# A transformer trunk layer on one core: the first feed-forward projection as a product of seven block products, with the engines' order written out

## The chip, the core and the metric

The kernel runs on one core of a Trainium2 chip. The metric is the device time of one execution in microseconds (us). Before the change it is 1105.56 us, the median of three runs from 1104.16 to 1106.84. A difference under 0.2% (2.2 us) is taken as none.

Engines are named as in the profile: PE (TensorE matmul), PEld (TensorE weight load), DVE (VectorE), ACT (ScalarE), POOL (GpSimd), SP (SyncE, which issues the loads).

## What is computed

One trunk layer with shared weights for 512 latent and 128 context tokens, 640 in all, model width 1024, feed-forward width 2816, float32. The part that the change touches is the second half of the layer:

```python
x = x + gate1 * (merged @ w_out)
h = modulate(x, norm2_w, shift2, scale2)       # RMSNorm(x) * (1 + scale2) + shift2
a, up = jnp.split(h @ w_ffn_in, 2, axis=-1)    # 1024 -> 2 x 2816
a = dwconv3(a, ffn_conv_w, ffn_conv_b)         # three taps along the tokens
x = x + gate2 * ((jax.nn.silu(a) * up) @ w_ffn_out)
```

Both groups of tokens end with a final RMSNorm. The vectors gate1, shift2, scale2 and gate2 come from products of a small condition vector with `w_ada`.

## The kernel before, in words

**Number format.** A float32 operand is held as two `F32R` tiles, `hi` (an ACT copy) and `lo` (operand minus hi, a DVE subtraction), and a product takes three matmuls: hi*hi, hi*lo and lo*hi. `wload` (line 117) and `wcols` (line 130) load 512 KB of weights from SP into a tile `raw` (three buffers), then make `whi` and `wlo` (four buffers each). `mm` (line 141) issues a matmul; where `pinned` is set, `pin` keeps the order of the program text on PE, and the other engines' instructions are placed by the scheduler.

**PSUM.** Eight banks: `bank2` (line 103) hands out pairs of banks in a turn of three, `bank1` single banks in a turn of two.

**Output projection.** For each of five blocks `t` of 128 tokens, `out_steps(t)` (line 1013) multiplies `mg` with `w_out` in 8 contraction blocks, three matmuls each, and both column halves: 48 matmuls of 512 columns. The first two blocks alternate. Behind the matmuls DVE multiplies by gate1, adds to `x2[t]`, ACT squares, and DVE scales by the reciprocal root. `modulate(t)` (line 1033) turns the block with eight PE transposes, applies scale2 and shift2 (four operations on DVE, four on ACT) into `h32`, and splits it into `h2[0]` and `h2[1]`. It stands inside the matmuls of the next block, behind its sixth contraction block.

**First feed-forward projection.** The 640 tokens are two halves of 320 (`HALF`), the contraction is 8 blocks of 128. For each of 22 tiles `i` of 128 columns, `ffn_tile` (line 1083) has `ffn_proj` (line 985) compute the tile of `a` (`pfa`) and the tile of `up` (`pfu`): per tile and operand 8 blocks x 3 matmuls x 2 halves = 48 matmuls of 128x320. Three half projections (`ffn_half`, `early`) run before the last `modulate`. ACT copies `pfa` to `av` and applies the middle tap into `cv`; DVE adds the other two taps (four `scalar_tensor_tensor`, 511 and 127 columns), ACT applies silu, DVE multiplies by `pfu`, ACT and DVE split the product into hi and lo of the gated tile (`gA`, `gB`).

**Second feed-forward projection.** Tiles go in two groups of 11 (`GRP`, line 1074). After a group, its gated tiles are multiplied with `w_ffn_out` for two column halves `hf`, in five accumulators `acc` of 512 columns, and DVE adds `acc * g2` to `x2`. `gate2` (line 1076) gets gate2 by `ada_acc` (line 208): 1024 rows of `w_ada` times the condition, 16 `scalar_tensor_tensor` on DVE per column half; one step of it runs behind each of the first tiles. In the very last half `finish` (line 1102) applies the final norm and stores.

Of the kernel before, what the change touches and what calls it, by code (L numbers as in the profile page):

```python
# [67 lines left out]
def trunk_kernel(ctx: ExitStack, tc: tile.TileContext, a: dict, o: list):  # L68
# [72 lines left out]
    def mm(out, s, m, start, stop):  # L141
        pin(nc.tensor.matmul(out, s, m, start=start, stop=stop))  # L142
# [65 lines left out]
    def ada_acc(pool, col, hf, name):  # L208
# [3 lines left out]
        acc = pool.tile([P, 2, 512], F32, tag="acc", name=f"acc_{name}{hf}", bufs=2)  # L212
# [3 lines left out]
        for u in range(4):  # L216
            raw = wpool.tile([P, 2, 512], F32, tag="raw", name=f"raw_{name}{hf}{u}", bufs=3)
            nc.sync.dma_start(raw, w_ada[2 * u * P:(2 * u + 2) * P, c0:c0 + 512].rearrange("(k p) n -> p k n", p=P))
            for ki in range(2):
                for c in range(2):  # L220
                    nc.vector.scalar_tensor_tensor(acc[:, c, :], raw[:, ki, :], sc[:, c, 2 * u + ki:2 * u + ki + 1],  # L221
                                                   acc[:, c, :], ALU.mult, ALU.add)
# [16 lines left out]
    def rows_cols(pool, ps):  # L239

        rows = pool.tile([8, 512], F32, tag="n2rows", name="n2rows", bufs=1)
# [731 lines left out]
    h2 = mg  # L973
    tail = ctx.enter_context(tc.tile_pool(name="tail", bufs=1, reuse_waits="tile"))
    x2 = [tail.tile([P, D], F32, tag=f"x2_{t}", name=f"x2_{t}") for t in range(NT)]
    g2 = [tail.tile([P, D], F32, tag=f"g2_{c}", name=f"g2_{c}") for c in range(2)]

    def ffn_half(i, u):

        w = wcols(w_fi, u * FF + i * P, P, 0, KD, f"f{'au'[u]}{i}")  # L980
        ps = bank2(f"pf{'au'[u]}{i}")
        proj(ps, w, h2, KD, halves=(0,))
        return ps, w

    def ffn_proj(i, u):
        if (i, u) in early or i < 2:
            ps, w = early.get((i, u)) or ffn_half(i, u)
            proj(ps, w, h2, KD, halves=(1,))
            return ps
        w = wcols(w_fi, u * FF + i * P, P, 0, KD, f"f{'au'[u]}{i}")  # L990
        ps = bank2(f"pf{'au'[u]}{i}")
        proj(ps, w, h2, KD)
        return ps

    early = {}
    with tc.tile_pool(name="wo", bufs=1, reuse_waits="tile") as wo:
# [3 lines left out]
        woB = [wo.tile([P, 3, D], F32R, tag=f"woB{i}", name=f"woB{i}") for i in range(2)]  # L1000

        def wo_of(i, k):
            return woA[i][:, k, :] if k < 5 else woB[i][:, k - 5, :]

        for k in range(KD):
            raw = wpool.tile([P, 1024], F32, tag="raw", name=f"raw_wo{k}", bufs=3)
            nc.sync.dma_start(raw, w_out[k * P:(k + 1) * P, :])
            nc.scalar.copy(wo_of(0, k), raw)
            nc.vector.tensor_tensor(wo_of(1, k), raw, f(wo_of(0, k)), ALU.subtract)
# [3 lines left out]
        def out_steps(t):  # L1013
# [3 lines left out]
            for k in range(KD):  # L1017
                for i, (s, m) in enumerate(((0, 0), (0, 1), (1, 0))):
                    for b in range(2):
                        mm(ps[:, b, :], mg[s][:, k, ts], wo_of(m, k)[:, b * 512:(b + 1) * 512],  # L1020
                           k == 0 and i == 0, k == KD - 1 and i == 2)
                if k % 2 and k < KD - 1:
                    yield
            y = Y2[t] = wo.tile([P, D], F32, tag="y", name=f"y{t}", bufs=2)
            for b in range(2):
                nc.vector.tensor_tensor(y[:, b * 512:(b + 1) * 512], ps[:, b, :], g1[b][:, t // 4, :], ALU.mult)
            nc.vector.tensor_tensor(x2[t], x2[t], y, ALU.add)
            ss = wo.tile([P, 1], F32, tag="ss", name=f"ss2_{t}", bufs=4)
            nc.scalar.activation(y, x2[t], AF.Square, accum_out=ss)
            r = rstd_of(wo, ss, f"n2_{t}")  # L1030
            nc.vector.tensor_scalar(y, x2[t], r, None, ALU.mult)

        def modulate(t):
            c, ts, y = t // 4, slice(t * P, (t + 1) * P), Y2[t]
            h32 = wo.tile([P, KD, P], F32, tag="h32", name=f"h32_{t}", bufs=1)
            for q in range(2):
# [3 lines left out]
                for j in range(4):  # L1040
                    kk = 4 * q + j
                    src, s_, b_ = pt[:, j * P:(j + 1) * P], modc["sc2"][:, kk, c:c + 1], modc["sh2"][:, kk, c:c + 1]
                    if j % 2:
                        nc.scalar.activation(h32[:, kk, :], src, AF.Identity, bias=b_, scale=s_)
                    else:
                        nc.vector.tensor_scalar(h32[:, kk, :], src, s_, b_, ALU.mult, ALU.add)
            n = KD if t < NT - 1 else KD // 2
# [154 lines left out]
```

## Time and profile before

| | us |
|---|---|
| median of three runs | 1105.56 |
| the profiled execution | 1108.31 |
| its span, first to last instruction | 1106.5 |
| PE busy in the span | 1071.1 (97%) |
| DVE busy | 701.2 (63%) |
| ACT busy | 486.5 (44%) |
| POOL busy | 163.0 (15%) |
| mean granted clock of TensorE, share of full | 0.991 |

The span begins with the first instruction and ends with the last; the profiled execution's own time is 1.8 us longer. Busy time of an engine is the union of its instructions. A matmul's row shows its whole latency, and matmuls overlap, so the pace of a run of matmuls is read from the chain, which gives the length of a stretch and how many matmuls it holds. In an idle note such as `[6.60 <-DVE ks L578]` the engine stood for 6.60 us until the named instruction ended.

### The profile page before, as it was taken

Reading aid. Unit: us, or ns where it says so; the run is one execution under the profiler, and the core shown is the slowest. Engines: PE = TensorE matmul, PEld = TensorE weight load, DVE = VectorE, ACT = ScalarE, POOL = GpSimd, SP = SyncE. Lnnn points to the kernel's source line nnn. Section 1 sums busy time; section 2 is a strip of 40 time slices with the busy share of each in tenths; the row PEclk is TensorE's granted clock in tenths of the full one; section 3 lists DMA queues with packets and bytes.
Section 4 is the critical chain, followed back from the end, with each engine's and each line's share of the span. In section 5 each row is a group of like instructions: output and inputs, shape, how many; then the busy total and the mean of one; then the engine's idle time right before and its main releaser. Section 6 shows DMA issues by size and latency. Waiting matters only on the chain.

```text
span 1106.5 us, 16752 instructions
## 1 busy us (share of the span) xinstructions
PE 1071.1 (97%) x6811; PEld 1006.3 (91%) x6811; DVE 701.2 (63%) x1041; ACT 486.5 (44%) x783; POOL 163.0 (15%) x160
## 2 busy tenths in 40 slices
PE   6988999999999999999999999999999999999997
PEld 4787899999999999999998899999988999999886
DVE  5968988988877577787756567564414444444164
ACT  8636667667665552222334444333311233333133
POOL 4444324323222630000000000000000000000020
PEclk9898999999999999999999999999999999999999
DMA  9830212112111124555565024241222222222212
GB/s 311 228 97 27 84 32 65 48 37 66 41 42 58 55 81 152 171 156 150 153 220 161 1 80 141 86 133 58 86 76 76 87 77 76 77 77 68 67 39 95
DMA packets 128478, 106.10 MB, mean 96 GB/s; under 512 B 4173, under 2 KB 110205, under 8 KB 128402
## 3 DMA queue, kind: packets, MB, share of 16 engines
q1 hardware_dynamic: 126450, 101.93, 29.9%
q0 software_dynamic: 1232, 1.80, 0.8%
q8 instruction: 53, 0.87, 0.3%
q10 hardware_dynamic: 720, 1.31, 0.3%
q14 instruction: 23, 0.19, 0.1%
HBM read 101.36 MB, written 3.67 MB: 95 GB/s over the span
## 4 chain that ended last, share of the span: by engine, by line
PE 80%; DVE 11%; ACT 4%; issue 2%; SPq 1%; DMA 1%; ACTq 0%; DVEq 0%
PE pfa L142 14%; PE pfu L142 14%; PE acc L142 13%; PE ps_g L142 10%; PE psyb L142 5%; PE pso L142 5%; PE psk L142 3%; PE psu L142 3%; PE psya L142 3%; PE s L142 2%; PE po L142 2%; PE psq L142 2%; DVE nm L667 2%; PE psv L142 2%; PE pat L145 1%
## 5 line engine op out<-in xcount | busy, mean ns | idle before, releaser
L142 PE MATMUL pfu<-mg,whi_fu 128*128 128x320 f32 x704 | 134.1, 308 | 0.0
L142 PE MATMUL pfa<-mg,whi_fa 128*128 128x320 f32 x704 | 134.1, 308 | 0.0
L142 PEld LDWEIGHTS pfa<-mg,whi_fa 128*128 128x128 f32 x704 | 110.9, 188 | 0.4
L142 PEld LDWEIGHTS pfu<-mg,whi_fu 128*128 128x128 f32 x704 | 110.7, 188 | 0.0
L142 PE MATMUL acc<-whi_fo,gA 128*128 128x512 f32 (+1 forms) x336 | 100.9, 379 | 0.0
L142 PE MATMUL ps_g<-hT,whi_g 128*128 128x320 f32 x512 | 96.7, 311 | 0.0
L142 PE MATMUL pfu<-mg,wlo_fu 128*128 128x320 f32 x352 | 82.2, 307 | 0.0
L142 PE MATMUL pfa<-mg,wlo_fa 128*128 128x320 f32 x352 | 82.2, 307 | 0.0
L142 PEld LDWEIGHTS ps_g<-hT,whi_g 128*128 128x128 f32 x512 | 80.2, 188 | 2.0 <-issue 1.5
L126 DVE TENSOR_TENSOR wlo_fo<-raw_fo,whi_fo 128x1024 fp32r<-128x1024 f32 (+1 forms) x24 | 27.3, 1145 | 80.8 <-ACT whi_fo L125 80.8
L669 ACT ACTIVATE p<-s,nm 128x640 f32<-128x640 f32 (+1 forms) x80 | 56.6, 709 | 40.0 <-DVE nm L667 39.4
L142 PEld LDWEIGHTS acc<-whi_fo,gA 128*128 128x128 f32 x336 | 62.1, 188 | 12.1
L126 DVE TENSOR_TENSOR wlo_fa<-raw_fa,whi_fa 128x1024 fp32r<-128x1024 f32 x22 | 26.9, 1224 | 66.3 <-ACT whi_fa L125 66.3
L1176 POOL TENSOR_TENSOR x<-x,fw 128x512 f32<-128x512 f32 x5 | 6.9, 1372 | 419.0 <-ACT sq L1175 419.0
L142 PE MATMUL psv<-whi_v,hT 128*128 128x256 f32 x320 | 66.4, 288 | 0.0
L125 ACT CAST whi_fo<-raw_fo 128x1024 fp32r<-128x1024 f32 (+1 forms) x24 | 23.3, 978 | 96.3 <-PE acc L142 71.3
L667 DVE TENSOR_REDUCE nm<-s 128x1 f32<-128x640 f32 (+1 forms) x80 | 56.5, 709 | 12.4 <-PE s L142 11.0
L142 PE MATMUL acc<-wlo_fo,gA 128*128 128x512 f32 (+1 forms) x168 | 63.7, 379 | 0.0
L125 ACT CAST whi_fa<-raw_fa 128x1024 fp32r<-128x1024 f32 x22 | 23.1, 1050 | 84.8 <-PE pfa L142 61.7
L221 DVE SCALAR_TENSOR_TENSOR acc_g<-raw_g,silu,acc_g 128x512 f32<-128x512 f32 x64 | 44.5, 746 | 24.8 <-DMA raw_g<-in_w_ada_dram 24.7
L142 PEld LDWEIGHTS pfu<-mg,wlo_fu 128*128 128x128 f32 x352 | 59.4, 188 | 0.0
L142 PEld LDWEIGHTS pfa<-mg,wlo_fa 128*128 128x128 f32 x352 | 59.4, 188 | 0.0
(337 smaller groups left out, 2576.3 us busy)
## 6 DMA issues: line engine op xcount, KB each, us to landing
raw_fa<-in_w_ffn_in_dram SPq DMA_DIRECT2D x22, 512.0 KB
raw_fu<-in_w_ffn_in_dram SPq DMA_DIRECT2D x22, 512.0 KB
raw_fo<-in_w_ffn_out_dram SPq DMA_DIRECT2D x20, 512.0 KB
raw_g<-in_w_in_dram SPq DMA_DIRECT2D x16, 512.0 KB
raw_g<-in_w_ada_dram SPq DMA_DIRECT2D x16, 512.0 KB
araw_sh<-in_w_ada_dram SPq DMA_DIRECT2D x8, 512.0 KB
araw_sc<-in_w_ada_dram SPq DMA_DIRECT2D x8, 512.0 KB
raw_v<-in_w_in_dram SPq DMA_DIRECT2D x8, 512.0 KB
```

Source lines behind the costliest of these rows:

```text
L125: nc.scalar.copy(hi[:, :n], rv)
L126: eng.tensor_tensor(lo[:, :n], rv, f(hi[:, :n]), ALU.subtract)
L142: pin(nc.tensor.matmul(out, s, m, start=start, stop=stop))
L145: pin(nc.tensor.transpose(out, x, ident))
L221: nc.vector.scalar_tensor_tensor(acc[:, c, :], raw[:, ki, :], sc[:, c, 2 * u + ki:2 * u + ki + 1], acc[:, c, :], ALU.mult, ALU.add)
L667: nc.vector.tensor_reduce(nm[:, i:i + 1], s, AX.XY, ALU.max, negate=True)
L669: nc.scalar.activation(p.rearrange("p (b n) -> p b n", b=s.shape[1]), s, AF.Exp, bias=nm[:, i:i + 1], accum_out=z[:, i:i + 1])
L1176: nc.gpsimd.tensor_tensor(x2[t][:, hs], x2[t][:, hs], fw[:, hs], ALU.mult)
```

## The change

1. The first projection is one product of blocks of two by two: the weight tile of `a` (k blocks 0 to 3 and 4 to 7) and that of `up` (the same), against `h` cut into k blocks 0 to 3 and 4 to 7 and token halves 0 and 1. It takes seven block products of 12 matmuls (4 k blocks x 3) of 128x320, numbered 1 to 7 in `product`, in place of eight. The sums on the token side are made once in `modulate` (`e1` to `e4`, kept in `h2` and in the new tile `hx`). The sums on the weight side are made per tile by POOL (`sums`, four operations of 512 columns). Per tile the weights take four hi/lo pairs (`hilo` 1 to 4: three of 1024 columns and one of 512). Sums of the products are made in PSUM where they can be (`pa` collects 1, 6, 7, 4; `pc` 5 and 3) and by DVE (`add2`, `add7`, `add3`).
2. DVE, ACT and POOL instructions of this stage go through `Pin`, which keeps them in the order of the text. `start` writes out the first three tiles, `cycle` the others.
3. The tiles go in groups of 8, 7 and 7. The last two products of a group's last tile stand behind the first blocks of the second projection, and `prepare` readies the next group's first tile in its last block.
4. `gate2` is stepped twice behind each block of the second projection of group 0; half of its sums go to ACT and POOL (`part`). The load of the final norm's weight `fw`, issued by POOL, moves from the start of the stage to the second projection of the last group.
5. The output projection of blocks 2 to 4 goes one PSUM bank after the other (`by_half`), so that `half(0)` follows its first bank. `modulate(t-1)` stands behind contraction block 8 of the first bank (behind block 7 for the last), `modulate(0)` behind block 1.

The core of the diff:

```diff
+    dve, act, pool = Pin(nc.vector), Pin(nc.scalar), Pin(nc.gpsimd)
...
+    def load(i, u, dst=None):
+        raw = R[i, u] = dst if dst is not None else wpool.tile([P, KD, P], F32, tag="raw", ..., bufs=3)
+        nc.sync.dma_start(raw, w_fi[:, c0:c0 + P].rearrange("(k p) n -> p k n", p=P))
+    def sums(i, b, dst=None):
+        ra, ru = R[i, 0], R[i, 1]
+        s = S[i, b] = dst if dst is not None else pools["ffn"].tile([P, KD, P], F32, tag="s", ...)
+        if b == 0:
+            pool.tensor_tensor(s[:, :4, :], ru[:, :4, :], ru[:, 4:, :], ALU.add)
+            pool.tensor_tensor(s[:, 4:, :], s[:, :4, :], ra[:, :4, :], ALU.subtract)
+        else:
+            pool.tensor_tensor(s[:, :4, :], ra[:, 4:, :], S[i, 0][:, 4:, :], ALU.subtract)
+            pool.tensor_tensor(s[:, 4:, :], ra[:, :4, :], ru[:, :4, :], ALU.subtract)
+    def hi(i, n):
+        src = {1: lambda: R[i, 0], 2: lambda: S[i, 0], 3: lambda: S[i, 1], 4: lambda: R[i, 1][:, 4:, :]}[n]()
+        if n < 4:
+            w = [wpool.tile([P, KD, P], F32R, tag=t, ...) for t in ("whi", "wlo")]
+            for p, k0 in zip(((1, 2), (5, 6), (3, 7))[n - 1], (0, 4)):
+                W2[i, p] = [x[:, k0:k0 + 4, :] for x in w]
+        act.copy(w[0], src)
+    def lo(i, n, eng=dve):
+        eng.tensor_tensor(l, src, f(h), ALU.subtract)
+    def product(i, *ps):
+        for p in ps:
...
+            out = {1: pa, 6: pa, 7: pa, 4: pa, 5: pc, 3: pc, 2: PB.get(i)}[p]
+            (wh, wl), (ah, al) = W2.pop((i, p)), h_block(p)
+            for k in range(4):
+                for n, (w, x) in enumerate(((wh, ah), (wh, al), (wl, ah))):
+                    mm(out, w[:, k, :], x[:, k, :], p in (1, 2, 5) and k + n == 0, k == 3 and n == 2, p in (6, 7, 4, 3))
...
         def modulate(t):
+            free = dve if t == NT - 1 else pool
...
+            dve.tensor_tensor(e1, b12, h1[:, :4, cs], ALU.subtract)
+            dve.tensor_tensor(e2, b22, e1, ALU.subtract)
+            split_to(h2[0][:, :4, c2], h2[1][:, :4, c2], e1)
+            free.tensor_tensor(e3, b22, b12, ALU.subtract)
+            yield
+            split_to(hx[0][:, :4, cs], hx[1][:, :4, cs], e2)
+            split_to(h2[0][:, 4:, c2], h2[1][:, 4:, c2], b22, free)
+            yield
+            free.tensor_tensor(e4, h1[:, 4:, cs], e2, ALU.subtract)
+            split_to(hx[0][:, 4:, cs], hx[1][:, 4:, cs], e[:, 8:, :n], free)
...
+            for n in out_steps(t, True):
+                if n == (7, 7, 6)[t - 2]:
+                    each(modulate(t - 1))
+                elif t == 2 and n == 0:
+                    each(modulate(0))
+                elif t == NT - 1 and n in (2, 10):
+                    hilo(n // 8, 1, pool)
+                elif t == NT - 1 and n == 14:
+                    hi(2, 1)
...
+        lo(2, 1, pool)
+        product(0, 1, 2)
+        product(1, 1)
+        copy1(0, spare[0][:, 7, :])
+        add2(0)
+        sums(0, 0, room(0, 2))
+        rest = modulate(NT - 1)
+        next(rest)
+        product(2, 1)
+        product(1, 2)
+        hilo(0, 2)
+        sums(0, 1, room(1, 2))
+        next(rest)
+        product(2, 2)
+        hilo(0, 3)
+        each(rest)
...
+    def cycle(i, first, end):
+        j, n = (i - 1 if i > first else None), (i + 1 if i < end else None)
...
+        product(i, 1, 2)
+        do(j, lambda j: product(j, 7))
+        do(j, add3)
+        do(j - 1 if j is not None and j > first else None, glo)
+        do(j, conv)
+        copy1(i)
+        do(n, sums, 0)
+        do(n, hi, 2)
+        add2(i)
+        do(n, lo, 2)
+        do(j, silu)
+        do(j, add7)
+        do(j, glu2)
+        do(n, hi, 1)
+        product(i, 5)
+        do(n, sums, 1)
+        copy5(i)
+        do(n, lo, 1)
+        do(n, hi, 4)
+        do(n, lo, 4)
+        product(i, 6)
+        if i + 2 <= end:
+            load(i + 2, 0)
+        copy6(i)
+        do(n, hi, 3)
+        do(j, lambda j: product(j, 4))
+        do(j, glu1)
+        do(n, lo, 3)
+        product(i, 3)
+        if i + 2 <= end:
+            load(i + 2, 1)
...
+    def start():
+        product(0, 5, 6)
+        load(2, 1)
+        copy5(0)
+        sums(1, 0)
+        sums(1, 1)
+        hilo(1, 2)
+        copy6(0)
+        product(0, 3, 7)
...
+        hilo(0, 4)
+        hilo(1, 4)
+        product(1, 5, 6)
...
+        product(0, 4)
...
+        product(1, 3, 7)
...
+        product(2, 5, 6)
...
+        product(1, 4)
...
+        product(2, 3)
...
+        out2 = blocks()
+        next(out2)
+        product(end, 7)
+        add7(end)
+        glu2(end)
+        next(out2)
+        product(end, 4)
+        glu1(end)
+        glo(end)
+        each(out2)
```

`add2`, `add7`, `add3` and `glu1` are one DVE operation of 320 columns with one operand in PSUM, `glu2` one of 320 columns and `glo` one of 640 with both in SBUF. `copy1`, `copy5` and `copy6` are ACT copies of 320 columns from PSUM. `conv` is the old middle tap on ACT and the old four operations on DVE. `hilo` is `hi` and `lo`.

## Rows read from the trace of the kernel before

**Rows 1.** The page, engines: busy us, share of the span, instructions

```profile
PE 1071.1 (97%) x6811; PEld 1006.3 (91%) x6811; DVE 701.2 (63%) x1041; ACT 486.5 (44%) x783; POOL 163.0 (15%) x160
```

**Rows 2.** The page, chain that ended last, shares of the span by line

```profile
PE pfa L142 14%; PE pfu L142 14%; PE acc L142 13%; PE ps_g L142 10%; PE psyb L142 5%; PE pso L142 5%; PE psk L142 3%; PE psu L142 3%; PE psya L142 3%; PE s L142 2%; PE po L142 2%; PE psq L142 2%; DVE nm L667 2%; PE psv L142 2%; PE pat L145 1%
```

**Rows 3.** Groups of `pfa` (`pfu` has the same): count, busy us, mean ns, idle

```profile
L142 PE MATMUL pfa<-mg,whi_fa 128*128 128x320 f32 x704 | 134.1, 308 | 0.0
...
L142 PE MATMUL pfa<-mg,wlo_fa 128*128 128x320 f32 x352 | 82.2, 307 | 0.0
```

**Rows 4.** Chain in order of time: start us, length us, matmuls in it

```profile
611.31 11.11 PE pso L142 x48
...
709.12 7.04 PE pfa L142 x48
...
912.42 6.99 PE pfa L142 x48
```

**Rows 5.** Tiles 11 to 21: length, busy of PE, PEld, DVE, ACT, POOL, clock

```profile
870.50:1024.20 153.70, 153.70 (x1057) 153.70 (x1057) 67.78 (x95) 53.87 (x66) 0.00 (x0) 1.00 0.26 78
```

**Rows 6.** The same stretch, groups of DVE: count, busy us, mean ns

```profile
L126 DVE TENSOR_TENSOR wlo_fu<-raw_fu,whi_fu 128x1024 fp32r<-128x1024 f32 x10 | 12.2, 1218 | 0.0
L1091 DVE SCALAR_TENSOR_TENSOR cv<-av,vcol,cv 128x511 f32<-128x511 f32 (+1 forms) x22 | 11.2, 550 | 1.7 <-ACT cv L1089 1.5
...
L1098 DVE TENSOR_TENSOR gA<-cv,gA 128x640 fp32r<-128x640 f32 x8 | 6.6, 819 | 0.0
```

**Rows 7.** Groups of ACT by form: count, busy us, mean ns, idle

```profile
L125 ACT CAST whi_fu<-raw_fu 128x1024 fp32r<-128x1024 f32 x22 | 23.1, 1048 | 45.3 <-PE pfu L142 18.1 <-PE pfa L142 14.5 <-PE acc L142 5.7
L1089 ACT ACTIVATE cv<-pfa,vcol 128x640 f32<-128x640 f32 x22 | 19.6, 889 | 0.0
...
L1095 ACT ACTIVATE cv<-cv 128x640 f32<-128x640 f32 x22 | 16.3, 739 | 47.3 <-DVE cv L1093 47.2
...
L736 ACT COPY u<-psu 128x320 f32<-128x320 f32 x4 | 1.7, 419 | 0.0
```

**Rows 8.** Timeline, POOL with DVE: operands all in SBUF, then DVE reading PSUM

```profile
1066.90 1.29 POOL L1176 TENSOR_TENSOR x<-x,fw 128x512 f32<-128x512 f32 x1 [1.44 <-ACT sq L1175]
...
1066.92 1.81 DVE L1172 TENSOR_TENSOR x<-x,yr 128x512 f32<-128x512 f32 x1
...
73.99 2.85 POOL L126 TENSOR_TENSOR wlo_q<-raw_q,whi_q 128x1024 fp32r<-128x1024 f32 x1
76.81 1.74 POOL L541 TENSOR_TENSOR ry_k<-ry_k,cos 128x512 f32<-128x512 f32 x1
...
74.50 2.89 DVE L542 TENSOR_TENSOR rsh_k<-rsh_k,sin 128x512 f32<-128x512 f32 x1
...
355.46 2.68 POOL L748 TENSOR_TENSOR s<-s 128x669 f32<-128x669 f32 x2 [0.42 <-DVE u L759]
...
355.49 2.35 DVE L693 TENSOR_TENSOR tl<-pat,th 128x1024 fp32r<-128x1024 f32 x2
```

**Rows 9.** Operations of line 1172: shortest, middle and longest in ns

```profile
L1172 DVE TENSOR_TENSOR x<-x,yr x15: 681/689/1812, 832.7 to 1072.4; 128x512 f32<-128x512 f32 x15
```

**Rows 10.** A weight load: its issue, then microsecond stretches ending in DMA share, GB/s

```profile
914.51 0.37 SPq L122 DMA_DIRECT2D raw_fa<-in_w_ffn_in_dram  x1
...
917.00:918.00 1.00, 1.00 (x9) 1.00 (x8) 0.00 (x0) 0.00 (x0) 0.00 (x0) 1.00 0.56 167
918.00:919.00 1.00, 1.00 (x9) 1.00 (x8) 0.00 (x0) 0.00 (x0) 0.00 (x0) 1.00 0.00 0
```

**Rows 11.** Timeline, `modulate` near the end of the output projection

```profile
634.84 1.78 DVE L1046 TENSOR_SCALAR h<-pt,sc,sh 128x128 f32<-128x128 f32 x4 [2.68 <-PE pt L145]
```

**Rows 12.** PE after a long idle time, and engines and clock in two stretches

```profile
86.45 0.60 PE L142 MATMUL s<-ks,qd 128*128 128x320 f32 x1 [6.60 <-DVE ks L578]
...
80.00:85.00 5.00, 0.00 (x0) 0.00 (x0) 4.87 (x7) 3.13 (x5) 3.57 (x3) 0.89 0.00 1
85.00:90.00 5.00, 3.54 (x14) 3.58 (x15) 4.68 (x6) 1.31 (x4) 0.63 (x1) 0.50 0.00 0
```

More of the change, by code (lines that the diff above doesn't have):

```diff
@@ new lines, in copy1, with add2, copy5, copy6 @@
+    def copy1(i, dst=None):
+        AV[i] = dst if dst is not None else pools["ffn"].tile([P, TOK], F32, tag="av", name=f"av{i}")
+        act.copy(AV[i][:, :HALF], PS[i][:, 0, :HALF])
+    def add2(i):
+        dve.tensor_tensor(AV[i][:, :HALF], AV[i][:, :HALF], PB.pop(i), ALU.add)
+    def copy5(i):
+        C22[i] = pools["ffn"].tile([P, HALF], F32, tag="c22", name=f"c22_{i}")
+        act.copy(C22[i], PS[i][:, 1, :HALF])
+    def copy6(i):
+        act.copy(AV[i][:, HALF:], PS[i][:, 0, :HALF])
@@ L1027, in out_steps @@
[L1027 to L1031, printed above, removed]
+                if n == len(order) - 1:
+                    continue
+                yield n
+                if n == KD - 1:
+                    half(0)
+            if not by_half:
+                half(0)
@@ new lines, in prepare, with do @@
+    def prepare(i):
+        load(i, 0)
+        load(i, 1)
+        sums(i, 0)
+        hilo(i, 1)
+        sums(i, 1)
+        hilo(i, 2)
+        hilo(i, 4)
+        load(i + 1, 0)
+        hilo(i, 3)
+        load(i + 1, 1)
+    def cycle(i, first, end):
+        j, n = (i - 1 if i > first else None), (i + 1 if i < end else None)
+        def do(tile, op, *args):
+            if tile is not None:
+                op(tile, *args)
+        product(i, 1, 2)
[29 more added lines that the diff above has]
+            load(i + 2, 1)
@@ new lines, in trunk_kernel, with blocks @@
+    later = gate2()
+    for g, (first, size) in enumerate(GROUPS):
+        end = first + size - 1
+        if g == 0:
+            start()
+        else:
+            gates_of(g)
+        for i in range(3 if g == 0 else first, end + 1):
+            cycle(i, first, end)
+        add3(end)
+        glo(end - 1)
+        conv(end)
+        silu(end)
+        def blocks():
+            for hf in range(2):
+                for _ in out2_steps(g, hf):
+                    yield
+                    if g == 0:
+                        next(later, None)
+                        next(later, None)
+        out2 = blocks()
[8 more added lines that the diff above has]
+        each(out2)
```

345 lines of the change are left out of this document (223 added, 122 removed).

## The prediction

> **What bounds the kernel now.** I read the page's engine line first: PE is busy for 97% of the span [rows 1]. Then the chain that ended last: `pfa` and `pfu`, the two operands of the first feed-forward projection, hold 28% of it [rows 2]. Their groups give the count: 704 + 352 matmuls for `pfa`, as many for `pfu`, 2112 in all, with no idle time in front [rows 3]. A matmul's row shows latency (308 ns), so the pace comes from the chain in order of time: 48 matmuls in 7.04 or 6.99 us, 146.7 or 145.6 ns each [rows 4]. Last, the stretch of tiles 11 to 21: PE works 153.70 of 153.70 us at full clock, 13.97 us a tile, while DVE works 67.78, ACT 53.87 and POOL nothing [rows 5]. So only PE's work costs time here, and the question is whether the other engines' new work stays under what is left of PE's.
>
> **Matmuls removed: 38.5 us less.** Seven products of 12 matmuls for 22 tiles are 1848, 264 fewer than 2112. At 145.6 to 146.7 ns that is 38.4 to 38.7 us. A product takes 1.75 us, a tile 12.24.
>
> The Trainium skill, "TensorE: Matmul & The Clock Gate", Back-to-back issue gap, states some 81 ns a matmul at 128 columns and 131 at 512 in a sustained stream; a straight line between them is an estimate of 106 ns at 320, which would make the saving 28 us and the end 1104. The trace has 231 ns at 512 columns (48 in 11.11 us) [rows 4], so its own pace is used.
>
> **The repeating cycle: 11.9 us more.** Per tile DVE gets three subtractions of 1024 columns at 1.22, one of 512 at 0.69, the convolution (four operations, 2 x 11.2 / 11 = 2.04 a tile), one of 640 at 0.82, and five of 320, by the step from 512 to 640 some 0.49 each [rows 6, 9]: 9.7 us, against 6.1 before. ACT gets three copies at 1.05, one of 512 (some 0.6), a tap at 0.89, silu at 0.74, the gated copy (some 0.73) and three copies of 320 at 0.42: 7.4 [rows 7]. POOL gets four sums at 1.29: 5.2 [rows 8]. Each is under 12.24, but they don't run side by side. Where POOL and a DVE operation with both operands in SBUF meet, the second stands still: DVE began 0.02 us behind POOL, took 1.81 in place of 0.69 and ended 0.54 after it; POOL, caught the same way, ended 1.16 after DVE [rows 8, 9]. DVE reading PSUM isn't held: two such operations took 2.35 us under two of POOL [rows 8].
>
> I walk one cycle with these (0 is the start of product 1; *n* is the next tile, *j* the one before). The loop settles at 13.1 us. The last weights of *n* go into the buffer that `lo(n-1,1)` freed near 11.0 of the cycle before; a load takes some 3.1 us from issue (914.51 to about 917.6) [rows 10], so they land near 1.2. DVE ends `lo(.,3)` at 0.4, `add3` at 0.8, `glo` at 1.5; ACT's tap lets the convolution begin at 1.7. POOL takes the port at 1.5, and its four sums then alternate with the four taps: first sum until 2.65, taps of 0.55, 0.55, 0.17, 0.17 (the last two by length), three sums of 1.15: the convolution ends at 7.5, where 2.04 would have ended it near 3.8. `add2` ends at 7.9, `lo(n,2)` at 9.1, `add7` at 9.55. Product 4 adds onto the bank that `add7` reads, and PE stands before it from 8.75 (five products): 0.85 us. Nothing else stops PE: `hi(n,1)` must wait for product 6 to give back its `whi` buffer, ends at 9.9, and `lo(n,1)` at 11.05 is in time for 13.1; `copy5` ends at 10.3, before product 3. Queued behind the late convolution are on ACT silu (until 8.3), on DVE all the rest; POOL's sums delay nobody but DVE. Only tiles with a successor in their group do sums: 4 + 5 + 5 = 14, so 11.9 us. Bounds: 0, if the sums fall into DVE's waits and PSUM operations; 2.35 a tile, 33 us, if DVE's 9.7 and POOL's 4 x 1.16 never overlap and the waits on ACT (0.25) stay. I take the walk, since the rows prove both the blocking and the free PSUM operations.
>
> **The start: 13 us more.** (0 is the end of the output projection.) Block 3 is transposed 7 us earlier, and DVE and ACT apply scale and shift in 1.78 [rows 11] plus latency. Then POOL does `e3`, a subtraction and `e4`, 1.16 to 1.29 each, alternating with DVE and waiting twice for ACT; `e4` ends near 1.8. ACT's order puts its copy next (2.9), then a square, then `hi(1,1)` (4.75); POOL's two subtractions of 1024 at 2.3 (2.85 less the 0.5 until DVE let go, its next operation starting at 74.50 [rows 8]) end at 5.2 and 7.5. PE has only products 1 and 2 of tile 0, until 3.5: it waits 4.0 us for `lo(1,1)`. The last block's transposes and three products end at 15.4; on DVE scale and shift (1.8), four operations of 512 and `lo(0,2)`, alternating with four sums, end at 17.9: product 5 waits 2.5. In the 13 products that remain (22.7 us) DVE has about 22 us and POOL 8 to 12 sums between its operations; with half of them in the way that is some 6.5 us too long. Bounds: 4, if only the first wait is left; 20, if every sum is in the way.
>
> **Group ends: 1 us more** (0 to 3). The second projection keeps its matmuls. In a group's first cycle PE has five products, 8.75 us; DVE has 4.8 us of the tile and five pairs of 0.69 for the accumulators, 11.7, which the next cycle partly takes up. `prepare` has the last block and the ones before as cover.
>
> **At nothing.** Output projection bank by bank: 48 matmuls in 11.11 us show no idle time to win [rows 4]; `modulate` has 24 matmuls (5.5 us) as cover for a tail that I put at 4.6, and if that is gone each of four blocks costs up to 1. gate2 behind the second projection: 240 matmuls at 0.231 are 55 us, against POOL's 16 sums, 20.6 us, and SP's 16 loads there, each some 2 us of DMA time [rows 10]; if it slips, up to 3. `fw` moves behind POOL's last sums, one column half (24 us of matmuls) ahead of its first reader. SP issues the same loads in the first projection, in an order that only tightens the last one of each tile, walked above.
>
> **Sum.** -38.5 + 11.9 + 13 + 1 = -12.6. The profiled execution has 1108.3 (span 1106.5 and 1.8 around it), so 1095.7 there; it stands 2.7 above the median, and the median 1105.6 goes to 1093.0.
>
> **Rivals.**
> - *All of it hidden.* POOL's sums fall into DVE's waits, and the start costs 4: -34.5, 1071. For it: DVE and ACT have 5 us a tile free by count. Against: the blocked rows. 18%.
> - *The shared port sets the cycle (slower).* DVE and POOL alternate throughout, and a tile takes 14.6 us: 33 + 13 + 3 - 38.5 = +10.5, 1116. It decides from the point where a cycle passes 14.0, today's tile, as the start and the group ends eat the other 14 us. For it: 9.7 and 5.2 add to 14.9. Against: five of DVE's operations can't be held, four of them reading PSUM and one behind them. 18%.
> - *The clock falls in the start.* After 6.60 us without matmuls the next ran from 86.45 on at half clock; the stretch to 90 has 0.50 [rows 12]. Some 4.3 us at half cost 2.2. Two or three falls, with the start at 20 and the rest as above: near 1105, no change. Against: the waits walked are 4.0 and less. 10%. The Trainium skill, "TensorE: Matmul & The Clock Gate", HAM oscillation, says that idle gaps between bursts put the array back to half clock; the trace agrees at 6.60 us, and for 4 us no row that I use shows it.
> - *The change doesn't do what it says:* not in the count, since the loops issue 84 matmuls a tile; only the pace could differ, and operands and shapes stay.
>
> **How the numbers follow.** My forecast has 54%, from 1084 to 1102. Faster by over 0.2% (2.2 us, about what a measurement of this kernel can tell from none): 0.54 + 0.18 + a third of the clock case, 0.75. Within it: 0.06, most of the clock case. Slower: 0.19. For 8 in 10 the range goes from 1070, the hidden case, to 1113, into the slower one.
>
> **What would show it.** Right: 1848 matmuls on the seven products, PE standing 0.5 to 1.2 us before product 4 in tiles with a successor and not in a group's last; convolution operations on DVE of about 1.7 us mean for the 511 columns, and POOL's sums at 1.3 to 1.8; waits of 2 us and more before product 1 of tile 1 and product 5 of tile 0. Wrong: a steady cycle of 12.3 us (the port doesn't matter), or one over 14; PE waiting for DMA landings or for ACT's `copy5`; low clock behind the start.

## The result and the profile after

The changed kernel takes 1262.57 us (median of 4 runs, 1260.09 to 1267.28), the kernel before 1104.86 in the same series: a ratio of 1.143, 95% interval 1.139 to 1.147. The forecast was 1093 and its range ended at 1113.

The page's engine line, in the columns of [rows 1], and the chain by line, as in [rows 2]:

```profile
PE 1084.3 (86%) x6535; PEld 996.8 (79%) x6535; DVE 822.4 (65%) x1197; ACT 549.3 (44%) x911; POOL 335.6 (27%) x276
...
PE pf L156 11%; PE acc L156 7%; DVE cv L149 2%; PE pb L156 2%; ACT whi_f L149 1%; ACT cv L149 1%; ACT uh L149 0%; DVE av L149 0%; DVE wlo_fo L126 0%; ACT c L149 0%; ACT av L149 0%; DVE x L1341 0%; ACT whi_fo L125 0%; ACT acc L1277 0%; DVE yr L1275 0%
```

PE falls from 97% to 86%, and no other engine takes its place: DVE has 65%. So nothing is full; PE waits. The view of waits for PE says for what (us in all, times, longest), and the groups of the products, in the columns of [rows 3], say where:

```profile
PE pf L156 <- ACT av L149: 49.2, 33, 5.5
PE pf L156 <- ACT c L149: 38.8, 19, 4.9
PE pso L156 <- DVE y L149: 20.3, 3, 7.2
...
L156 PE MATMUL pf<-mg,whi_f 128*128 128x320 f32 x528 | 125.2, 325 | 51.6 <-ACT av L149 49.2
L156 PE MATMUL pf<-hx,whi_f 128*128 128x320 f32 x352 | 85.8, 332 | 38.8 <-ACT c L149 38.8
```

The three waits make 108.3 us. `pf` is the accumulator of the products, `av` and `c` are what ACT copies out of it, `y` is what DVE reads out of the output projection's accumulator `pso`. None of these stalls stood in the kernel before: its view of waits for PE is empty from 553 us on. The repeating cycle, one tile, in windows (length, busy of PE, PEld, DVE, ACT, POOL, granted clock), beside 13.97 us a tile before [rows 5]:

```profile
929.43:947.20 17.77, 13.06 (x86) 12.27 (x86) 9.21 (x14) 6.73 (x10) 5.66 (x5) 1.00 0.20 60
947.20:965.00 17.80, 13.09 (x86) 12.30 (x86) 9.21 (x14) 6.73 (x10) 6.18 (x5) 1.00 0.20 59
```

DVE with 9.21 us and ACT with 6.73 are near what the prediction counted (9.7 and 7.4). PE stands for 4.7 us in each cycle. The timeline of the first of these cycles, without the other matmuls, shows how (start, length, engine, and in brackets the idle time before and what ended it):

```profile
930.87 0.31 PE L156 MATMUL pf<-hx,wlo_f 128*128 128x320 f32 x1
931.22 0.49 DVE L149 TENSOR_TENSOR av<-av,pf 128x320 f32<-128x320 f32 x1 [4.08 <-PE pf L156]
...
931.74 0.92 ACT L149 ACTIVATE cv<-av,vcol 128x640 f32<-128x640 f32 x1 [6.26 <-DVE av L149]
932.57 0.40 ACT L149 COPY av<-pf 128x320 f32<-128x320 f32 x1
...
933.03 0.56 PE L156 MATMUL pf<-mg,whi_f 128*128 128x320 f32 x2 [1.84 <-ACT av L149]
...
935.62 1.03 ACT L149 CAST whi_f<-raw_fa 128x1024 fp32r<-128x1024 f32 x1
936.56 0.42 ACT L149 COPY c<-pf 128x320 f32<-128x320 f32 x1
...
937.03 0.56 PE L156 MATMUL pf<-hx,whi_f 128*128 128x320 f32 x2 [1.97 <-ACT c L149]
...
941.23 0.42 ACT L149 COPY av<-pf 128x320 f32<-128x320 f32 x1
...
941.70 0.56 PE L156 MATMUL pf<-mg,whi_f 128*128 128x320 f32 x2 [0.89 <-ACT av L149]
```

Read it as a chain. Product 7 ends at 931.18; only then does DVE's `add3` start, though the bank that it reads had been complete since before products 1, 2 and 7. ACT's tap waits for it, `copy1` stands behind the tap in ACT's written order, and product 5 waits for `copy1`, though it writes the other bank. The same happens at 937.03 (product 6 and `copy5`) and 941.70 (product 3 and `copy6`). The common thing is the tile: `PS[i]` is one tile of two banks. The output projection has it too, where the second bank's matmuls wait for DVE's reading of the first:

```profile
625.05 5.55 PE L156 MATMUL pso<-woA,mg 128*128 128x512 f32 x15 [7.20 <-DVE y L149]
646.07 5.29 PE L156 MATMUL pso<-woA,mg 128*128 128x512 f32 x15 [6.98 <-DVE y L149]
```

The end of each kernel from 553 us on (up to there the two profiles run alike), by windows:

| kernel | from 553 us, length | PE busy | PE idle | granted clock |
|---|---|---|---|---|
| before | 553.5 | 547.2 | 6.3 | 1.00 |
| changed | 705.2 | 563.2 | 142.0 | 0.92 |
| changed, banks apart (first experiment) | 602.7 | 536.1 | 66.6 | 0.96 |
| best version (last experiments) | 536.6 | 515.6 | 21.0 | 0.99 |

The table's clock is the mean granted clock as a share of full. The last three kernels run the same matmuls. So of the 168.6 us between the changed kernel and the best version 121.0 are idle time, and 47.6 the same work taking longer, with the clock at 0.92 in place of 0.99.

### The profile page after: what moved, and what is told of

It reads as the page before. It is cut to its first block, busy times and chain, and to the rows that moved or that the text cites. A ratio compares the mean times of both kernels' runs of the same rounds, so it can differ in the third digit from the quotient of the medians.

```text
span 1258.2 us, 16726 instructions
## 1 busy us (share of the span) xinstructions
PE 1084.3 (86%) x6535; PEld 996.8 (79%) x6535; DVE 822.4 (65%) x1197; ACT 549.3 (44%) x911; POOL 335.6 (27%) x276
## 5 line engine op out<-in xcount | busy, mean ns | idle before, releaser
L156 PE MATMUL pf<-mg,whi_f 128*128 128x320 f32 x528 | 125.2, 325 | 51.6 <-ACT av L149 49.2
L156 PE MATMUL acc<-whi_fo,g 128*128 128x512 f32 (+1 forms) x454 | 141.3, 389 | 5.7 <-DVE yr L1340 5.7
L156 PEld LDWEIGHTS pf<-mg,whi_f 128*128 128x128 f32 x528 | 91.1, 196 | 61.3 <-ACT av L149 58.1
L156 PE MATMUL pf<-hx,whi_f 128*128 128x320 f32 x352 | 85.8, 332 | 38.8 <-ACT c L149 38.8
L156 PEld LDWEIGHTS acc<-whi_fo,g 128*128 128x128 f32 x454 | 86.4, 192 | 23.6 <-DVE yr L1340 6.4
L156 PEld LDWEIGHTS pf<-hx,whi_f 128*128 128x128 f32 x352 | 62.7, 202 | 44.5 <-ACT c L149 44.3
L156 PE MATMUL acc<-wlo_fo,g 128*128 128x512 f32 (+1 forms) x227 | 88.5, 390 | 0.1
L156 PE MATMUL pf<-mg,wlo_f 128*128 128x320 f32 x264 | 84.5, 320 | 3.5 <-DVE wlo_f L149 3.5
L149 DVE TENSOR_TENSOR wlo_f<-s,whi_f 128x1024 fp32r<-128x1024 f32 x42 | 60.3, 1436 | 19.7 <-ACT whi_f L149 19.6
L686 DVE TENSOR_REDUCE nm<-s 128x1 f32<-128x640 f32 (+1 forms) x80 | 56.5, 710 | 12.4 <-PE s L156 11.0
L156 PE MATMUL ps_g<-hT,wlo_g 128*128 128x320 f32 x256 | 59.0, 312 | 0.4 <-DVE wlo_g L126 0.4
L156 PE MATMUL pso<-woA,mg 128*128 128x512 f32 x150 | 41.7, 437 | 20.3 <-DVE y L149 20.3
```

The lines of the kernel that those rows point to most:

```text
L149: pin(getattr(self.eng, op)(*args, **kw))
L156: pin(nc.tensor.matmul(out, s, m, start=start, stop=stop, skip_group_check=more))
L686: nc.vector.tensor_reduce(nm[:, i:i + 1], s, AX.XY, ALU.max, negate=True)
```

## The experiments

Times are medians in us, and where a ratio has an interval it stands beside it; a time without a count of runs is a single run. The four runs of the kernel with the banks apart spread over 8.0 us (1153.73 to 1161.69), so single runs that differ by less are not told apart. The kernel before took 1103.7 to 1107.0 beside these runs.

**Banks apart.** Each two-bank accumulator becomes two one-bank tiles from the output projection on. No instruction is added or moved.

```diff
+    psT = ctx.enter_context(tc.tile_pool(name="psT", bufs=3, space=PSUM, reuse_waits="tile"))
...
+    def banks(name):
+        return [psT.tile([P, 512], F32, tag=t, name=f"{name}{t}") for t in "ac"]
...
-                PS[i] = bank2(f"pf{i}")
-            pa, pc = PS[i][:, 0, :HALF], PS[i][:, 1, :HALF]
+                PS[i] = banks(f"pf{i}")
+            pa, pc = PS[i][0][:, :HALF], PS[i][1][:, :HALF]
...
-            ps = bank2(f"pso{t}")
+            ps = banks(f"pso{t}")
```

> Edit: from the output projection on, each two-bank accumulator becomes two one-bank tiles (three of each kind, as many banks as before); no instruction is added, removed or moved. Theory A (a matmul into one bank is held until the copy out of the other bank of the same tile is done, because the two share a tile): TensorE's waits behind av, c and y (49.2 + 38.8 + 20.3 = 108.3 us in the changed kernel) fall below 15 together, the repeating cycle goes from 17.78 us to 13 to 14, the granted clock rises from 0.949 to 0.98 or more, and the time lands between 1080 and 1140. Theory B (the written order of ACT alone holds TensorE, whichever tile the sums stand in): the waits stay under other names and the time stays over 1220. Theory C (the port shared by DVE and GpSimd is the cause): the cycle stays over 16 us and the time over 1200.

Measured: 1157.68 (4 runs), ratio to before 1.047, 1.043 to 1.052; 104.9 us off the changed kernel, and the waits behind `av`, `c <- ACT` and `y` of `pso` are gone. Theory A holds for the cause, but its sizes miss: the time lies 17.7 us above its span, the clock is 0.972, not 0.98, and of the fourteen full cycles three last 13.3 to 13.4 us, eight 13.9 to 14.4, two 15.8 to 16.0 and the first 19.7. Timeline and windows of this kernel:

```profile
918.37 0.45 PE L157 MATMUL pf12c<-mg,whi_f 128*128 128x320 f32 x2
...
918.95 0.42 ACT L150 COPY av<-pf12a 128x320 f32<-128x320 f32 x1
919.09 0.31 PE L157 MATMUL pf12c<-mg,wlo_f 128*128 128x320 f32 x1
...
872.81:887.02 14.21, 12.47 (x84) 12.21 (x84) 12.70 (x15) 6.84 (x12) 6.23 (x4) 1.00 0.25 75
887.02:901.28 14.26, 12.47 (x84) 12.21 (x84) 12.76 (x15) 6.83 (x11) 5.85 (x4) 1.00 0.27 75
...
764.64 0.56 PE L157 MATMUL pf5a<-hx,uh 128*128 128x320 f32 x2 [1.64 <-DVE c L150]
```

The last row is a wait before product 4, which is left. The first three rows show `copy6` reading bank `a` of tile 12 while product 3 writes bank `c`: the chip lets both go on at once, so the wait came from how the program tracks its tiles. The Trainium skill, "PSUM — Partial Sum Buffer", PSUM bank collisions raise a hardware error, says that two engines on different banks run clean; these rows agree. The Trainium skill, "Perfetto Trace Analysis", Matmuls, advises to rotate matmul groups through different banks so that the evacuation of one overlaps the next group; the changed kernel did alternate between the two banks of a tile, and the timeline above shows no overlap between them, because both belonged to one tile.

**Apart in one half only**, with the same edit in the feed-forward products alone, then in the output projection alone.

> Edit: the accumulators are taken apart from the first feed-forward product on; the output projection keeps its two-bank tiles. Theory A: the waits behind av and c (88.0 us) go, the three of 7 us behind y (20.3) stay, and the output projection's low clock with them; the time is that of the first run plus 20 to 45 us. Theory B or C: within 20 us of the changed kernel's 1262.

> Edit: the reverse, the accumulators are taken apart in the output projection alone. Theory A: the waits behind y (20.3 us) go, the ones behind av and c stay at 80 to 95 us, the cycle stays at 17 to 18 us, and the time falls by 20 to 45 us from 1262. Theory B or C: within 10 us of 1262.

Measured: 1170.76 and 1251.15. The output projection is worth 13.1 and 11.4 us, less than the 20 to 45 expected: its 20.3 us of waits go, but with all banks apart the transposes then wait 4.0 us for `y`, against 0.6 in the changed kernel. The rest, 92 us, is in the products. The second run also settles a rival: the new tiles come from a pool with `reuse_waits="tile"`, which the old ones lack. There the products' two-bank tiles come from such a pool too, and the waits stay, as does the cycle of 17.8 us:

```profile
PE pf L157 <- ACT av L150: 49.3, 33, 5.6
PE pf L157 <- ACT c L150: 39.1, 19, 5.4
```

So it is the tile that counts, not the pool.

**Copies first**, tiles shared:

```diff
-        do(n, hi, 1)
         product(i, 5)
...
         copy5(i)
+        do(n, hi, 1)
...
-        do(n, hi, 4)
-        do(n, lo, 4)
         product(i, 6)
...
         copy6(i)
+        do(n, hi, 4)
+        do(n, lo, 4)
```

> Edit: two-bank tiles kept; in the repeating cycle the copy out of product 5's bank goes ahead of one weight split on ACT, and the copy out of product 6 ahead of another. Theory A: product 6 starts some 0.9 us earlier and product 3 some 0.9 us earlier in each of 17 cycles, so the cycle falls from 17.78 to about 16 us and the time by 15 to 35 us. Theory B says the same of the wait behind ACT, theory C no change over 5 us. If the weight splits, now later, hold the next tile's products, the gain is smaller and a wait behind whi or wlo takes its place.

Measured: 1238.59, 24.0 us less, as theory A says, and theory B with it. Behind the first, the cycles last 15.7 to 18.0 us with a median of 16.8, where about 16 was expected. It is no remedy.

**No sums.** On top of the banks apart, GpSimd's weight sums are left out, and the splits read the first weight tile in their place.

```diff
     def sums(i, b, dst=None):
...
-            pool.tensor_tensor(s[:, :4, :], ru[:, :4, :], ru[:, 4:, :], ALU.add)
...
+        S[i, b] = R[i, 0]
```

> Edit, on top of the kernel with the banks apart (1157.7 us, repeating cycle 13.36 us): GpSimd's weight sums of the feed-forward tiles are left out, so the splits read the first weight tile in their place (part of the computation is left out). Theory P (DVE's four convolution instructions, 5.2 to 5.8 us in place of 2.2, are slow because they alternate with GpSimd's sums, and TensorE waits before product 4 for that): convolution 2.2 to 2.4 us, the waits behind c before product 4 (0.9 to 1.9 us in each cycle) gone, cycle 12.3 to 12.6 us, time 1112 to 1142. Rival D (DVE's list is too long by itself): cycle 13 or more, time within 8 us of 1157.7.

Measured: 1114.55, 43.1 us less. The convolution's two forms (count, busy us, mean ns), with the sums in the kernel with the banks apart:

```profile
L150 DVE SCALAR_TENSOR_TENSOR cv<-av,vcol,cv 128x511 f32<-128x511 f32 x42 | 54.8, 1305 | 6.0 <-ACT cv L150 5.3
L150 DVE SCALAR_TENSOR_TENSOR cv<-av,vcol,cv 128x127 f32<-128x127 f32 x42 | 39.4, 938 | 0.6
```

and without them, with two of its cycles:

```profile
L150 DVE SCALAR_TENSOR_TENSOR cv<-av,vcol,cv 128x511 f32<-128x511 f32 x42 | 32.6, 775 | 7.0 <-ACT cv L150 6.4
L150 DVE SCALAR_TENSOR_TENSOR cv<-av,vcol,cv 128x127 f32<-128x127 f32 x42 | 15.6, 372 | 0.6
...
860.36:872.65 12.29, 12.29 (x86) 12.29 (x85) 9.12 (x15) 6.96 (x10) 0.00 (x0) 1.00 0.31 87
872.65:884.94 12.29, 12.29 (x86) 12.29 (x85) 9.13 (x15) 6.97 (x11) 0.00 (x0) 1.00 0.30 86
```

Theory P holds: four instructions take 2 x 1305 + 2 x 938 = 4.5 us with GpSimd at work and 2.3 without, and the cycle is PE's own 12.29 once they are short. The 43.1 us can hold more than the alternation, since the splits no longer wait for sums either.

**Bank by bank undone**, on top of the banks apart.

```diff
-            for n in out_steps(t, True):
-                if n == (7, 7, 6)[t - 2]:
+            for n in out_steps(t):
+                if n == 5:
                     each(modulate(t - 1))
...
```

> Edit, on top of the kernel with the banks apart: the output projection goes back to both banks alternating in the last three blocks, and the turns of the finished blocks to the same places among the matmuls as in the kernel before. Theory: bank by bank wins nothing here once the tiles are apart, since the waits that are left in this stage (4.0 us behind y and 3.3 us behind h before transposes) are those of the elementwise chain; the time moves by no more than 8 us either way. Rival: bank by bank is worth its place; the time rises by 8 to 20 us, because the products then start behind a longer chain.

Measured: 1161.08, 3.4 more, within the spread of the kernel that it started from: it could not be told here.

**Only PE's order written**, on top of the banks apart:

```diff
     class Pin:
...
-                pin(getattr(self.eng, op)(*args, **kw))
+                getattr(self.eng, op)(*args, **kw)
```

> Edit, on top of the kernel with the banks apart: only TensorE keeps the written order; ACT, DVE and GpSimd are left to the planner. Theory: the written order of these three is not what costs, since the waits left are behind DVE's own work; the time stays within 15 us of 1157.7. Rival (the fixed order costs): the time falls by more than 15 us and the waits in the start (18 us from 654 to 690) go.

Measured: 1124.97, 32.7 us less. The theory missed: the order written for ACT, DVE and GpSimd costs, and the rival's part is right.

**Sums on DVE**, on top of the banks apart:

```diff
-    def sums(i, b, dst=None):
+    def sums(i, b, dst=None, pool=dve):
...
-        do(n, sums, 0)
-        do(n, hi, 2)
+        do(n, hi, 1)
...
         product(i, 5)
-        do(n, sums, 1)
+        do(n, sums, 0)
         copy5(i)
-        do(n, lo, 1)
+        do(n, hi, 2)
+        do(n, sums, 1)
...
```

> Edit, on top of the kernel with the banks apart: in the repeating cycle and at the ends of groups the sums go from GpSimd to DVE, behind the gating, and the splits that read them behind those; the sums of the start stay on GpSimd. Theory P: four sums cost DVE about 4 x 0.68 = 2.7 us, no more than the alternation cost the convolution (5.2 to 5.8 less 2.2), and product 4's operand is ready 3 us early; cycle 12.3 to 12.8 us, time 1122 to 1147. Rival D: DVE with some 12 us of work per cycle becomes the bound; cycle 13 us or more, time 1150 or more.

Measured: 1134.26, 23.4 us less, the cycle 12.4. One long stall is left in the waits, before product 4 of tile 6 in the last cycle of the first group; with the sums on GpSimd it was 4.5 us:

```profile
PE pf6a L157 <- DVE c L150: 10.2, 1, 10.2
```

DVE there runs the second gate's sums and the splits of the second projection's weights between the taps of the convolution, slowed by GpSimd's additions for that gate. The prediction had gate2 "at nothing".

**Only PE's order written, tiles shared.** The edit of two runs before, on the changed kernel itself.

> Edit, on the changed kernel itself (two-bank tiles kept, 1262.6 us): only TensorE keeps the written order; ACT, DVE and GpSimd are left to the planner. Theory A (the shared tile makes the waits, the written order of ACT makes them long): the planner puts the copies out of the banks earlier, TensorE's waits behind av and c fall from 88 us to 30 to 60, those behind y (20.3) fall too, and the time is 1170 to 1230, over the 1125 of the same edit with the banks apart. Rival B (the written order alone is the cause): the waits behind av and c go below 15 us and the time comes within 15 us of 1125. Rival (the order has no part in it): over 1245.

Measured: 1140.55, far under what theory A gave and 15.6 over the run with the banks apart, just outside rival B's 15; its waits behind `av` and `c` make 20.8, where rival B has under 15. Both miss, and the run is the most useful one: with ACT's copies where the planner wants them, the shared tile costs PE only

```profile
PE pf L156 <- ACT c L149: 18.1, 19, 2.9
```

some 0.95 us each time in the mean, of which the copy itself takes 0.42. Tile and written order are dear together: taking either away gives back 105 or 122 us, both 138.

**Order and sums**, the two edits together; then **the second gate's sums on DVE** as well (first pair of lines), and **the start left free**, on top of the sums on DVE with the orders written (the rest):

```diff
-            for acc in ada_acc(ffn, 5 * D, hf, "g2", "s", "yr"):
+            for acc in ada_acc(ffn, 5 * D, hf, "g2", "s"):
...
-                pin(getattr(self.eng, op)(*args, **kw))
+                ins = getattr(self.eng, op)(*args, **kw)
+                if fixed[0]:
+                    pin(ins)
...
+        fixed[0] = True
         for i in range(3 if g == 0 else first, end + 1):
```

> Edit: banks apart, only TensorE's order written, and all weight sums on DVE. If the two remedies act on different losses (order: 1157.7 to 1125.0; sums: 1157.7 to 1134.3) the time is 1095 to 1112; if they act on the same loss (DVE held by GpSimd in the start and at the ends of the groups) it is 1115 to 1130.

> Edit, on top of the run before this one: the sums of the second gate go back to DVE for both halves, so that ACT's scalings and GpSimd's additions of that stage go. Theory P (GpSimd's additions, 1.8 us each, slow DVE at the end of the first group): the wait of TensorE before the last product 4 of that group is shorter and the time falls by 2 to 10 us. Rival: DVE's own list at that place grows by as much; within 3 us, or slower.

> Edit, on top of the banks apart with the sums on DVE in the cycle (1134.3 us): ACT, DVE and GpSimd keep the written order from the first repeating cycle on, and are left to the planner in the output projection and the start. Theory: the written order costs most in the start, where TensorE waits some 20 us in 600 to 720 us, so the time falls by 8 to 20 us to 1114 to 1126. Rival: it costs in the cycles and at the ends of the groups; within 5 us of 1134.

Measured: 1103.45, 1093.65 and 1122.26, each in its theory's span. The remedies add up, 32.7 and 21.5; gate2 is worth 9.8, and the written order costs 12.0 in the output projection and the start.

**ACT alone free**, tiles shared, on the changed kernel.

```diff
-    dve, act, pool = Pin(nc.vector), Pin(nc.scalar), Pin(nc.gpsimd)
+    dve, act, pool = Pin(nc.vector), nc.scalar, Pin(nc.gpsimd)
```

> Edit, on the changed kernel itself (two-bank tiles kept, 1262.6 us): ACT alone is left to the planner; TensorE, DVE and GpSimd keep the written order. Theory A2 (the copies that release TensorE are late because ACT's written order puts them behind work that waits for DVE): the waits behind av and c fall from 88 us to 20 to 45, the repeating cycle from 17.78 to 13.5 to 15 us, and the time is 1140 to 1195. Rival (DVE's written order is what holds: ACT, free or not, waits for DVE): over 1220.

Measured: 1225.43, 37 less only. Theory A2 missed, and the time is the rival's. The waits behind `av` are nearly gone (2.7), but those behind `c` stay, and others come up:

```profile
PE pf L156 <- ACT c L1077: 34.2, 19, 6.3
PE pf L156 <- DVE c L149: 28.7, 18, 5.0
```

So ACT's list alone was not the cause. The timeline above has another wait in the chain: DVE's `add3` stands until product 7 has ended.

**The loop cut by program order**, tiles shared, all orders written; then with the copies first as well.

```diff
         product(i, 1, 2)
-        do(j, lambda j: product(j, 7))
         do(j, add3)
         do(j - 1 if j is not None and j > first else None, glo)
         do(j, conv)
+        do(j, lambda j: product(j, 7))
         copy1(i)
```

> Edit, on the changed kernel itself (two-bank tiles and all written orders kept; the order of instructions on each engine stays as it was): product 7 of a tile is put in the program behind the addition and the convolution of that tile, so the addition no longer reads a bank of a tile that product 7 has yet to write. Theory L (the cycle of 17.78 us is a loop through TensorE: product 7, addition, tap, copy, product 5, copy, product 6): the addition starts 5 us earlier, ACT's 6.26 us wait for it goes, TensorE's wait behind av before product 5 (1.84 us) goes, the cycle is 13.5 to 15.5 us, and the time 1190 to 1225. Rival (the wait of product 5 and 6 for copies is what holds, wherever the addition stands): cycle over 17 us, time over 1245.

> Edit: the one above and the earlier one that puts two copies ahead of weight splits on ACT (which took 24 us from the changed kernel). Theory L: with the loop gone each product that shares a tile waits only for the copy itself, some 0.9 us before product 6; cycle 13.2 to 14.2 us, time 1175 to 1205, 10 to 20 us under the run before this one. Rival: the copies no longer matter once the addition is early; within 4 us of it.

Measured: 1216.12 and 1198.86; behind the first, the cycles have medians of 16.0 (15.3 to 17.5) and 14.7 (13.7 to 16.4). In the first, no engine's sequence changes, only what `add3` has to wait for, and 46.5 us go: theory L holds. Of the waits behind `av`, only the 0.9 us before product 3 are left:

```profile
PE pf L156 <- ACT av L149: 13.5, 16, 0.9
```

Both medians stay some 0.5 us over their spans; the first kernel's timeline shows why:

```profile
913.49 0.47 DVE L149 TENSOR_TENSOR av<-av,pf 128x320 f32<-128x320 f32 x1
...
915.34 4.14 DVE L149 SCALAR_TENSOR_TENSOR cv<-av,vcol,cv 128x511 f32<-128x511 f32 x4
...
921.14 0.42 ACT L149 COPY c<-pf 128x320 f32<-128x320 f32 x1
...
921.62 0.56 PE L156 MATMUL pf<-hx,whi_f 128*128 128x320 f32 x2 [2.29 <-ACT c L149]
```

The convolution now meets the sums (4.14 us; 2.19 in the changed kernel, where the loop kept the two apart), and silu, a weight split and `copy5` stand behind it on ACT.

**The best version**: banks apart, only PE's order written, the weight sums and the second gate's sums on DVE; then without bank by bank.

> The version with the banks apart, only TensorE's order written, the weight sums and the second gate's sums on DVE (1093.65 in one look), against the kernel before. If the change's own idea holds once its waits are gone, the ratio is 0.985 to 0.993 with an interval that leaves out 1; if that look was a lucky one, 0.995 or more.

> Edit, on top of the best version: both banks alternate in all five blocks of the output projection, as in the kernel before. Theory (bank by bank is worth nothing or little): within 4 us of 1093.65. Rival (it is worth its place, because the elementwise chain of a block's first bank runs beside the second): slower by 5 to 12 us.

Measured: 1094.83 (5 runs, 1091.33 to 1096.64), ratio 0.9914, 0.9898 to 0.9930: faster than the kernel before, by 9.6 us. Its page and cycles:

```profile
PE 1036.4 (95%) x6535; PEld 967.7 (89%) x6535; DVE 841.7 (77%) x1301; ACT 544.8 (50%) x895; POOL 184.8 (17%) x172
...
862.79:875.08 12.29, 12.29 (x86) 12.29 (x85) 11.57 (x21) 7.16 (x11) 0.00 (x0) 1.00 0.29 87
875.08:887.36 12.28, 12.28 (x86) 12.28 (x85) 9.85 (x15) 7.90 (x11) 0.00 (x0) 1.00 0.29 92
```

Without bank by bank 1100.99: 6.2 us above that median, within its rival's 5 to 12, and 4.4 above the highest of the five runs. It is a single run, but the trace has the wait that the rival names: PE stands 13.3 us in place of 5.2 for the last block's normed rows before the transposes.

```profile
PE pt L160 <- DVE y L150: 16.0, 2, 13.3
```

## Why the prediction was wrong

The time lies 169.6 us above the forecast. Three of the prediction's own signs of being wrong came: a cycle over 14 us, PE waiting for `copy5`, and a low clock behind the start.

- **The step that failed** is "Nothing else stops PE", with "`copy5` ends at 10.3, before product 3". The walk let a bank be written as soon as its own readers were done. In the program a matmul into one bank of `PS[i]` waits for readers of the other, and a reader of one bank waits for matmuls into the other that stand before it in the program. That made `add3`, walked at 0.8 of the cycle, wait for product 7 and start at 5.4 (931.22 in a cycle that began at 925.79), and closed a loop through PE: 17.78 us where 13.1 was walked. Priced at 0, it cost 104.9 us with the written order of all engines, and 15.6 with PE's alone. The same holds for "Output projection bank by bank", where the text feared 1 us a block and three blocks stood some 7 each. The diff showed the pattern: one tile, two banks, readers and writers alternating between them. "PE waiting for ACT's `copy5`" was listed as a sign of being wrong, but no rival was made of it.
- **The written order of ACT, DVE and GpSimd** has no term at all, not even among those put at nothing. It cost 32.7 us with the banks apart and 122.0 with the tiles shared.
- **The matmuls removed** hold as counted: a tile takes 12.28 to 12.29 us where the text has 12.24. From 553 us on PE is busy 31.5 us less in the best version than before; 38.5 was the term, and the best version's clock stands at 0.99.
- **The repeating cycle** had the right mechanism and too small a size. DVE's operations do alternate with GpSimd's sums, and PE does wait before product 4, but for 24.8 us in the 14 tiles that the term counts (kernel with the banks apart; 5.2 of them before product 4 of tile 2), where the term was 11.9. The walk gave the four taps 0.55, 0.55, 0.17 and 0.17 plus a sum each. That adds to 1.44 where its own count has 2.04: 0.55 is the mean of both forms [rows 6], taken for the long one. Alone the long ones measure 775 ns and the short ones 372, beside the sums 1305 and 938. At 14.2 us the usual cycle lies nearer the rival "the shared port sets the cycle" (14.6). The Trainium skill, "SBUF — State Buffer", SBUF: two separate sides, calls the port pair that DVE and GpSimd share a lock held for a whole instruction, not a split bandwidth; the rows agree, since the long form loses 530 ns in the mean (1305 less 775) and the short one, a quarter of its columns, 566 (938 less 372).
- **The start** was put at 13 us, at most 20; with the banks apart PE stands 27.6 us between 597 and 724, and 22.4 of these belong to it (the other 5.2 are those before product 4 of tile 2, counted above). The named waits are there (5.1 in product 1 of tile 1, 4.6 in product 5 of tile 0); the transposes' waits behind ACT and DVE (7.3) and those in product 4 of tiles 0 and 1 (3.1 and 2.4) were not walked. In the best version 8.1 us are left between 597 and 724.
- **Group ends and gate2**, 1 and 0: gate2 alone measured 9.8; between the two runs that differ in it alone, PE's wait before product 4 of tile 6 goes from 3.4 to 0.2 us and those of the second gate's own matmuls (`pb_g`) from 6.1 to 2.3. The group ends were not measured apart.
- **The clock** was a rival with 10%, for the start alone. It did fall, in the start and in some cycles (0.92 from 553 us on in the changed kernel), but on top of the waits, and the time that the rival gave, no change, did not come.
- That the best version lands within 2 us of the forecast is no merit of the forecast: it lacks four things that the changed kernel has.

What stays open: what the start's parts cost one by one; where the written order costs beyond the 12.0 us measured in the output projection and the start; and how much of the 47.6 us of slower matmuls is the clock, since a matmul behind a pause also shows a longer row.

## What to carry to other kernels

When a change makes engines alternate between two parts of one accumulator tile, ask what unit the program's waits are kept in, and give each part its own tile if readers of one are to run beside writers of the other. A written order lengthens such a wait by all that stands ahead of the instruction that releases it, as the tap and `add3` stood ahead of `copy1` here; before writing one for four engines, measure it for the bounding engine alone. And look at a saving's price on the idle engine: GpSimd's sums cost DVE's convolution 2.2 us a tile, and DVE does four of them itself in 2.75 (0.68 to 0.69 each).

## What had not been expected of the hardware

The pauses ahead of a fall of the clock can be short. In the kernel with the banks apart PE paused 1.08 and 3.47 us within 5 us, and then ran for 3.5 us at a granted clock of 0.56, most of it at the lower of the two levels, 1.2 GHz in place of 2.4: the pairs that take 0.46 us took 0.73. Timeline of PE, then two windows (clock behind POOL's busy time):

```profile
669.74 0.41 PE L157 MATMUL pf0c<-mg,whi_f 128*128 128x320 f32 x1 [1.08 <-DVE mg L150]
673.62 0.42 PE L157 MATMUL pf0c<-mg,wlo_f 128*128 128x320 f32 x1 [3.47 <-DVE wlo_f L150]
...
675.35 0.73 PE L157 MATMUL pf0c<-mg,whi_f 128*128 128x320 f32 x2
...
677.60 0.46 PE L157 MATMUL pf0a<-hx,whi_f 128*128 128x320 f32 x2
...
673.60:677.10 3.50, 3.48 (x14) 3.49 (x15) 2.90 (x4) 0.56 (x1) 0.00 (x0) 0.56 0.52 148
...
680.00:684.00 4.00, 4.00 (x29) 4.00 (x28) 2.92 (x5) 1.86 (x2) 2.60 (x2) 1.00 0.00 0
```

A single pause of under 2 us can do it, and a like one need not. The same kernel pauses 1.68, 1.74 and 1.79 us before product 4 of three tiles running, with no other pause in those cycles. The clock stays at 1.00 in the two cycles behind the first two pauses (windows under the first experiment); behind the third the pairs take 0.73 us for a while, and that cycle's clock is 0.89:

```profile
901.60 0.56 PE L157 MATMUL pf10a<-hx,uh 128*128 128x320 f32 x2 [1.79 <-DVE c L150]
...
903.27 0.73 PE L157 MATMUL pf10a<-hx,uh 128*128 128x320 f32 x2
...
901.28:916.20 14.92, 14.03 (x84) 13.76 (x84) 13.14 (x15) 6.95 (x11) 6.38 (x4) 0.89 0.24 70
```

The prediction set its rival aside because the waits walked were 4.0 us and less. In the changed kernel's cycles, with pauses of 1.84, 1.97 and 0.89 us, the clock mostly stays up: of the four cycles from 929.4 to 1000.0 three have 1.00, two of them in the windows above, and one has 0.90 (965.0 to 982.6).
